# A two-layer decoder trunk: the written order inside the middle passes of its MLPs is changed

## The chip, the core and the metric

The kernel runs on one core of a Trainium2 chip. The metric is device time in microseconds (us). A core has engines with queues of their own: TensorE (PE in the profile, PEld for its weight loads) multiplies matrices, VectorE (DVE) and ScalarE (ACT) work on tiles element by element, GpSimd (POOL) and SyncE (SP) here only issue transfers. Matrix products land in PSUM, which has eight banks; everything else lives in SBUF.

## The reference

256 tokens of width 2048 pass through two layers. Layer 0 mixes with a short gated convolution, layer 1 with multi-head latent attention; each mixer is followed by a squared-ReLU MLP of inner width 8192, and every sub-layer ends in a layer norm:

```
def sq_relu_mlp(x, w1, w2):
    return jnp.square(jax.nn.relu(x @ w1)) @ w2
...
        h = layer_norm(ALPHA * h + mix, ln_g[layer, 0], ln_b[layer, 0])
        h = layer_norm(ALPHA * h + sq_relu_mlp(h, mlp_w1[layer], mlp_w2[layer]),
                       ln_g[layer, 1], ln_b[layer, 1])
```
All inputs and outputs are float32. The change concerns the two MLPs alone.

## The kernel before

Float32 products are made from two halves: `split` writes `hi`, a rounded copy of a tile (ACT, L139), and `lo`, what the rounding left out (DVE, L140). A product is hi x hi + hi x lo + lo x hi. So every weight tile that comes from memory (512 KB, `load_raw`, issued by SP) needs one ACT cast and one DVE subtraction before PE can use it.

An MLP (`mlp`) goes over the 8192 inner columns in eight passes `q` of 1024, and each pass over eight units `m` of 128 columns. Pass 0 is treated on its own. From pass 1 on a loop of **slots** runs, one slot for each unit (`steps`, L89). A slot holds:

- the **unit**: 16 x 2 matmuls of the first weight matrix (`mm_run`, L255 and L259) into one PSUM bank called "unit" (in slots without a pair, "6" by turns). Its sum is taken off by `evacuate`, which calls `whole`: an ACT copy (L399) and a DVE addition (L400) into the tile `fp`, which holds two units;
- in most slots the products of a **pair** of weight tiles of the second matrix with the hidden values of the pass before (`products_of`, `fast_products`): seven products by Strassen's scheme, 21 matmuls (L340 to L343) into the seven other banks.

After every odd unit two units are whole. ACT applies ReLU and square (L842), `form` makes three sums for the seven left factors (DVE, L688 to L691), and `finish_pair` splits the factors into hi and lo (tiles `h1a`, `h1c`, `h3a`, `h3c`). For the last unit of a pass, DVE does ReLU and square itself (L804). There is one `fp` tile, so a split must be done before the next even unit's sum is written.

Weights are prepared one slot ahead. `singles` are the two halves of the next unit's weights, one cast and one subtraction each. A pair is prepared in five steps by `prepare`: step 1 issues its two loads and makes `raw_t` (L172); step 2 splits the first tile; step 3 makes two differences (L177, L179) and splits `raw_t`; step 4 splits the second tile; step 5 splits the half-wide `t`. The function `step(i)` takes one of these steps for pair `i`.

The seven banks belong to one half `g` of the output columns at a time. After the fourth pair of a half (slot m=0 of the next pass) they change hands: seven **moves**, each an ACT copy out of a bank (`put_back`, L653) and mostly one back in (`resume`, L738). A slot that begins with moves still to make is called `crowded`; that is m=1. In pass 7 `fold` adds up parts of the output on DVE (L661).

The order of the work is the order in which the loop writes it: `Order.keep` chains all instructions of a slot on PE, on DVE and on ACT one behind the other, each engine for itself. Transfers are issued by SP in the order written and wait for one of seven `raw` buffers.

Before, a usual slot was written as: step 1, singles, step 2, step 3, products, `evacuate`, step 4, step 5, and behind an odd unit ReLU and square, sums and split. The split of units 0 and 1 stood in m=2 ahead of the products, that of the last two units between steps 4 and 5 of m=7.

Of the kernel before, what the change touches and what calls it, by code (L numbers as in the profile page):

```python
# [12 lines left out]
AF = mybir.ActivationFunctionType  # L13
# [3 lines left out]
P = 128  # L17
W = 256 + 2
T = 256
# [3 lines left out]
NQ = 8  # L23
QC = FF // NQ // P
# [12 lines left out]
FAST = range(1, NQ - 1)  # L37
SHIFT = 5
# [18 lines left out]
def trunk(ctx: ExitStack, tc: tile.TileContext, xT, vecs, lead, w_first, w_in, w_out, w_kv, w_q, w_uk, w_uv,  # L57
          w_qn, w_qp, w_o, w1, w2, w2f, cosT, sinT, mask, ident, gb, out):
    nc = tc.nc
# [53 lines left out]
    class Banks:  # L113
# [15 lines left out]
        @classmethod  # L129
        def next(cls):  # L130
            cls.count += 1
            return (cls.count - 1) % (4 if cls.more is None else 8)

    state = {"next": 0}
    ready = {}

    def split(hi, lo, src):

        nc.scalar.copy(hi, src)  # L139
        return nc.vector.tensor_tensor(lo, src, hi.bitcast(F32), ALU.subtract)  # L140
# [12 lines left out]
    def prepare(i):  # L153

        if len(stream[i]) == 1:
            raw = loaded.pop(i) if i in loaded else load_raw(i, stream[i][0])
            hi, lo = ready[i] = parts(i)
            split(hi, lo, tiled(raw))
            yield
            return  # L160
        r1, r2 = (load_raw(f"{i}_{j}", src) for j, src in enumerate(stream[i]))
        t = raws.tile([P, 1024], F32, tag="raw", name=f"raw{i}_t")
        out = []

        def finished(r, name):
            hi, lo = parts(name)
            split(hi, lo, tiled(r))
            out.append((hi, lo))

        b22, (b21, b12) = r1[:, BW:], (r2[:, :BW], r2[:, BW:])  # L170
        two = "p (a c) -> p a c"
        nc.vector.tensor_tensor(t.rearrange(two, a=2), b12.unsqueeze(1).to_broadcast([P, 2, BW]),  # L172
                                r1.rearrange(two, a=2), ALU.subtract)
        yield
        finished(r1, f"{i}_1")
        yield
        nc.vector.tensor_tensor(b12, b22, t[:, :BW], ALU.subtract)  # L177
        t4 = r1[:, :BW]
        nc.vector.tensor_tensor(t4, b21, b12, ALU.subtract)  # L179
        finished(t, f"{i}_t")  # L180
        yield
        finished(r2, f"{i}_2")
        yield
        f = state["fast"].tile([P, 2, BW], F32R, tag="t4", name=f"t4_{i}", bufs=2)
        split(f[:, 0, :], f[:, 1, :], t4)
        b1, t13, b2 = ([[v.rearrange("p b c -> p (b c)")[:, o:o + BW] for v in w] for o in (0, BW)] for w in out)
        ready[i] = {"11": b1[0], "22": b1[1], "21": b2[0], "T2": b2[1], "T1": t13[0], "T3": t13[1],
                    "T4": [f[:, 0, :], f[:, 1, :]]}
        yield

    def size(i):

        return 1 if len(stream[i]) == 1 else 5

    begun, loaded = {}, {}

    def step(i):

        steps = begun.setdefault(i, [prepare(i), 0])
        if steps[1] < size(i):  # L200
            next(steps[0])
            steps[1] += 1
# [373 lines left out]
    for k0, k1 in pieces:  # L576
        half, at = k0 // 8, slice(k0 % 8, (k1 - 1) % 8 + 1)
# [41 lines left out]
    def mlp(idx, ln, blocks, fast, begin=None, extra=None, last=False):  # L619
# [64 lines left out]
        def form(u):  # L684

            a21, a11, a12, s1, s2, s4 = (u[:, i * P:(i + 1) * P] for i in (0, 1, 3, 4, 6, 7))
            two = u.rearrange("p (i c) -> p i c", c=P)
            nc.vector.tensor_tensor(s1, a21, u[:, 2 * P:3 * P], ALU.add)  # L688
            nc.vector.tensor_tensor(two[:, 5:7, :], two[:, 0:5:4, :], a11.unsqueeze(1).to_broadcast([P, 2, P]),
                                    ALU.subtract)  # L690
            nc.vector.tensor_tensor(s4, a12, s2, ALU.subtract)  # L691

        def forms(u):

            if q in FAST or last:
                form(u)

        def finish_pair(j, u):
            f = factors[j // 2][:, j % 2]
            at = slice(P, 8 * P) if q in FAST else slice(0, 8 * P) if last else slice(0, 2 * T)  # L700
            split(f[:, 0, at], f[:, 1, at], u[:, at])

        q = 0
# [38 lines left out]
        rows = {}  # L742

        moves = []

        def move(n):

            for _ in range(n):
                if moves:
                    o, g, on = moves.pop(0)  # L750
                    put_back(o, g, ps[o])
                    if on:
                        resume(o, 1 - g)
# [14 lines left out]
        slots, i = [], state["next"]  # L768
        for q, m, pair in steps(last):
            n = (2 if q < NQ else 0) + (pair is not None)  # L770
            slots.append((q, m, pair, list(range(i, i + n))))
            i += n
        order = Order()
        for s, (q, m, pair, own) in enumerate(slots):
            lone = pair is None
            following = slots[s + 1][3] if s + 1 < len(slots) else []
            pairs = [i for i in following if size(i) > 1]
            ahead = [i for i in range(state["next"], (following or own)[-1] + 1) if i not in own and i not in begun]
            if not pairs:
                ahead = [i for i in range(state["next"], own[-1] + 6) if i not in own and i not in begun]  # L780
                ahead = ahead[:next((k for k, i in enumerate(ahead) if size(i) > 1), len(ahead))]
            singles = [i for i in ahead if size(i) == 1]
            for i in singles:
                loaded[i] = load_raw(i, stream[i][0])
            if q == FAST[0] and m == SHIFT:
                sums = act.tile([P, 4, 2, BW], F32, tag="xres", name=f"sums{idx}")
                for o, _, _ in FACTORS:
                    resume(o, 1)
            if q < NQ:
                w = take(2, 0)  # L790
                at = "6" if lone and (m - SHIFT) % 2 else "unit"
                un = psum("ps_u", bank[at])
                mm_run([(w, un)], xhl, 0, NC, NC, turned=TURNED if TURN(q, m) else None)

            def evacuate():

                if q == NQ:
                    return
                if m % 2 == 0:
                    rows[m // 2] = fast.tile([P, 8 * P], F32, tag="fp", name="fp")  # L800
                u = rows[m // 2]
                whole(un, u[:, (m % 2) * T:(m % 2 + 1) * T])
                if m == QC - 1:
                    nc.vector.scalar_tensor_tensor(u[:, T:2 * T], u[:, T:2 * T], 0.0, u[:, T:2 * T], ALU.max, ALU.mult)  # L804

            crowded = len(moves) > 0
            for i in pairs:
                step(i)
            for i in singles:
                step(i)  # L810
                move(1)
            if crowded:
                evacuate()
            for i in pairs:
                step(i)
            move(len(moves))
            for i in pairs:
                step(i)
            if rows and m == 2:
                finish_pair(0, rows.pop(0))  # L820
            if pair:
                products_of(*pair)
            if not crowded:
                evacuate()
            if q < NQ and m == QC - 1:
                forms(rows[m // 2])
            move(1)
            for i in pairs:
                step(i)
            move(1)  # L830
            if q < NQ and m == QC - 1:
                finish_pair(m // 2, rows.pop(m // 2))
            for i in pairs:
                step(i)
            move(2)
            if q < NQ:
                if m % 2 or m == QC - 2:
                    u = rows.get(m // 2)
                    if m < QC - 1:
                        at = u[:, :T] if m == QC - 2 else u[:, :2 * T]  # L840
                        for function in (AF.Relu, AF.Square):
                            nc.scalar.activation(at, at, function)  # L842
                        if m % 2:
                            forms(u)
                            if m > 1 or lone:
                                finish_pair(m // 2, rows.pop(m // 2))
                if extra and q == FAST[0] and m < NB:
                    for t in range(2):
                        extra(block, m, t, spare[1 + (2 * m + t) % 3])
                if begin and q == FAST[0] and m < 4 and m % 2 == 0:  # L850
                    nc.gpsimd.dma_start(parked[:, 4 * m:4 * m + 8, :], held_x[0][:, 4 * m:4 * m + 8, :])
                if q == NQ - 1 and m:
                    for _ in range(3 if m >= SHIFT else 2):
                        next(folds, None)
            order.keep()
        move(len(moves))
        for _ in folds:
            pass
# [436 lines left out]
```

## Time and profile before

| | us |
|---|---|
| median of three runs | 2048.57 (2048.47 to 2050.03) |
| the profiled execution | 2049.0 |
| its span, first to last instruction | 2047.2 |
| PE busy (11050 matmuls) | 2000.4 |
| DVE busy | 1757.3 |
| ACT busy | 1308.1 |
| slots of layer 0, first unit to the next stage | 452.1 to 1019.6 |
| slots of layer 1, first unit to the next stage | 1418.5 to 2015.8 |

Rows of the profile give start and length in us, the engine, the line of the kernel, the operation, and the tiles written and read. A bracket at the end of a row tells how long the engine was idle before it and what ended that. Rows of a window give its bounds, its length, the busy time of PE, PEld, DVE, ACT and POOL with the number of instructions, the granted clock of PE, the DMA share and GB/s. Rows of waits give the engine and line that waited, for whom, us in total, times, and the longest.

### The profile page before, as it was taken

Reading aid. Unit: us, or ns where it says so; the run is one execution under the profiler, and the core shown is the slowest. Engines: PE = TensorE matmul, PEld = TensorE weight load, DVE = VectorE, ACT = ScalarE, POOL = GpSimd, SP = SyncE. Lnnn points to the kernel's source line nnn. Section 1 sums busy time; section 2 is a strip of 40 time slices with the busy share of each in tenths; the row PEclk is TensorE's granted clock in tenths of the full one; section 3 lists DMA queues with packets and bytes.
Section 4 is the critical chain, followed back from the end, with each engine's and each line's share of the span. In section 5 each row is a group of like instructions: output and inputs, shape, how many; then the busy total and the mean of one; then the engine's idle time right before and its main releaser. Section 6 shows DMA issues by size and latency. Waiting matters only on the chain.

```text
span 2047.2 us, 29648 instructions
## 1 busy us (share of the span) xinstructions
PE 2000.4 (98%) x11050; PEld 1733.2 (85%) x11050; DVE 1757.3 (86%) x2539; ACT 1308.1 (64%) x1915; POOL 5.7 (0%) x27
## 2 busy tenths in 40 slices
PE   9999999999999999999999999999999999999998
PEld 8888888987887878888889998898788788887876
DVE  8667677777999999999898988776899999999998
ACT  7444455576767767677656665566676776767754
POOL 0000000000000000000000000000000000000000
PEclk9999999999999999999999999999999999999999
DMA  9766666664555556555665534664455555565554
GB/s 344 207 193 186 188 192 179 195 205 144 201 190 202 189 188 204 190 191 195 219 243 166 182 118 153 179 192 154 147 192 192 199 192 193 193 204 194 185 177 164
DMA packets 107711, 389.99 MB, mean 190 GB/s; under 512 B 11952, under 2 KB 12720, under 8 KB 107056
## 3 DMA queue, kind: packets, MB, share of 16 engines
q1 hardware_dynamic: 106560, 383.79, 57.5%
q0 software_dynamic: 864, 4.19, 0.5%
q8 instruction: 86, 1.41, 0.3%
q14 instruction: 57, 0.47, 0.1%
q10 hardware_dynamic: 144, 0.13, 0.0%
HBM read 383.87 MB, written 4.19 MB: 190 GB/s over the span
## 4 chain that ended last, share of the span: by engine, by line
PE 54%; DVE 33%; ACT 7%; issue 5%; DMA 1%; DVEq 0%; ACTq 0%
DVE lo L140 15%; PE ps_l L255 13%; PE ps_l L259 7%; PE ps_u L255 5%; DVE lo_t L140 4%; DVE raw_t L172 3%; PE ps_u L259 3%; ACT hi L139 3%; DVE raw L177 2%; DVE raw L179 2%; DVE t L140 2%; PE ps_d L342 2%; PE ps_d L343 2%; PE ps_d L340 2%; PE ps_w L289 2%
## 5 line engine op out<-in xcount | busy, mean ns | idle before, releaser
L140 DVE TENSOR_TENSOR lo<-raw,hi 128x1024 fp32r<-128x1024 f32 x710 | 848.2, 1220 | 133.3 <-ACT hi L139 61.3
L139 ACT CAST hi<-raw 128x1024 fp32r<-128x1024 f32 x710 | 725.0, 1050 | 258.9 <-PE ps_l L255 102.1
L255 PE MATMUL ps_u<-xhl,hi 128*128 128x512 f32 x1792 | 634.5, 400 | 38.3 <-DVE fp L400 38.3
L259 PE MATMUL ps_u<-xhl,lo 128*128 128x256 f32 x1792 | 489.6, 282 | 0.0
L255 PEld LDWEIGHTS ps_u<-xhl,hi 128*128 128x128 f32 x1792 | 333.4, 190 | 121.1 <-DVE fp L400 53.2
L259 PEld LDWEIGHTS ps_u<-xhl,lo 128*128 128x128 f32 x1792 | 342.6, 191 | 11.6
L255 PE MATMUL ps_l<-xhl_a,hi 128*128 128x512 f32 x704 | 244.1, 393 | 0.0
L259 PE MATMUL ps_l<-xhl_a,lo 128*128 128x256 f32 x704 | 195.4, 279 | 0.0
L255 PEld LDWEIGHTS ps_l<-xhl_a,hi 128*128 128x128 f32 x704 | 132.1, 188 | 29.9
L259 PEld LDWEIGHTS ps_l<-xhl_a,lo 128*128 128x128 f32 x704 | 131.9, 188 | 0.2
L139 ACT CAST hi_t<-raw_t 128x1024 fp32r<-128x1024 f32 x100 | 105.1, 1051 | 41.9 <-DVE raw_t L172 41.2
L172 DVE TENSOR_TENSOR raw_t<-raw,raw 128x1024 f32<-128x1024 f32 x100 | 121.9, 1219 | 0.2 <-DMA raw<-in_w2f_dram 0.2
L140 DVE TENSOR_TENSOR lo_t<-raw_t,hi_t 128x1024 fp32r<-128x1024 f32 x100 | 121.9, 1219 | 0.0
L399 ACT COPY t<-ps_u 128x256 f32<-128x256 f32 x112 | 41.3, 369 | 110.2 <-PE ps_u L259 110.2
L255 PE MATMUL ps_l<-z,hi 128*128 128x512 f32 x240 | 82.4, 391 | 0.0
L842 ACT ACTIVATE fp<-fp 128x512 f32<-128x512 f32 (+1 forms) x112 | 64.9, 580 | 26.5 <-DVE fp L400 24.7
L400 DVE TENSOR_TENSOR fp<-ps_u,t 128x256 f32<-128x256 f32 x112 | 47.0, 420 | 35.7 <-ACT t L399 34.4
L289 PE MATMUL ps_w<-xd,hi 128*128 128x258 f32 x256 | 72.8, 284 | 0.0
L288 PE MATMUL ps_w<-xd,lo 128*128 128x258 f32 x256 | 72.3, 282 | 0.0
L287 PE MATMUL ps_w<-xd,hi 128*128 128x258 f32 x256 | 72.3, 282 | 0.0
L179 DVE TENSOR_TENSOR raw<-raw 128x512 f32<-128x512 f32 x100 | 69.2, 692 | 3.5
L255 PE MATMUL ps_l<-oT,hi 128*128 128x512 f32 x208 | 71.3, 391 | 0.0
(361 smaller groups left out, 3900.0 us busy)
## 6 DMA issues: line engine op xcount, KB each, us to landing
raw<-in_w_dram SPq DMA_DIRECT2D x312, 512.0 KB, 4.2
raw<-in_w2f_dram SPq DMA_DIRECT2D x200, 512.0 KB, 4.3
raw<-in_w_in_dram SPq DMA_DIRECT2D x88, 512.0 KB, 4.4
raw<-in_w_out_dram SPq DMA_DIRECT2D x32, 512.0 KB, 4.3
raw<-in_w_o_dram SPq DMA_DIRECT2D x32, 512.0 KB, 4.2
raw<-in_w_kv_dram SPq DMA_DIRECT2D x10, 512.0 KB, 6.0
raw<-in_w_q_dram SPq DMA_DIRECT2D x8, 512.0 KB, 4.0
raw<-in_w_uk_dram SPq DMA_DIRECT2D x8, 512.0 KB, 4.3
```

The lines of the kernel that those rows point to most:

```text
L139: nc.scalar.copy(hi, src)
L140: return nc.vector.tensor_tensor(lo, src, hi.bitcast(F32), ALU.subtract)
L172: nc.vector.tensor_tensor(t.rearrange(two, a=2), b12.unsqueeze(1).to_broadcast([P, 2, BW]), r1.rearrange(two, a=2), ALU.subtract)
L179: nc.vector.tensor_tensor(t4, b21, b12, ALU.subtract)
L255: nc.tensor.matmul(ps, w[blk // 8][0][:, blk % 8, :], x, start=first, stop=False)
L259: nc.tensor.matmul(ps[:, :T], w[blk // 8][1][:, blk % 8, :], x[:, :T], start=False, stop=last)
L287: nc.tensor.matmul(ps[:, :W], hi, x[k][:, :W], start=k == 0, stop=False)
L288: nc.tensor.matmul(ps[:, :W], lo, x[k][:, :W], start=False, stop=False)
L289: nc.tensor.matmul(ps[:, :W], hi, x[k][:, W:], start=False, stop=k == NC - 1)
L399: nc.scalar.copy(t, ps[:, T:])
L400: nc.vector.tensor_tensor(out, ps[:, :T], t, ALU.add)
L842: nc.scalar.activation(at, at, function)
```

## The change

It touches the loop of slots only.

- `evacuate` comes ahead of step 3: a usual slot is now written as step 1, singles, (products), step 2, `evacuate`, step 3, step 4, step 5.
- Splits of factors are put on a list `due` and written in the next slot, behind its first single (or behind step 1 where there are no singles). For the last two units of a pass the three sums stand right behind `evacuate`. What is left on the list is written after the loop.
- Moves: one behind each of `evacuate`, step 3, step 4 and step 5; in a crowded slot all that are left stand ahead of step 2.
- Before the first pair: in the last slot but two ahead of it (`far`, slot m=3 of pass 1) steps 1 to 3 of that pair are written at the slot's end.
- In pass 7 the folds are taken five to a slot from m=5 on (layer 0), or one to a slot from m=1 on (layer 1).

```
-        def finish_pair(j, u):
+        def finish_pair(j, u, of):
             f = factors[j // 2][:, j % 2]
-            at = slice(P, 8 * P) if q in FAST else slice(0, 8 * P) if last else slice(0, 2 * T)
+            at = slice(P, 8 * P) if of in FAST else slice(0, 8 * P) if last else slice(0, 2 * T)
             split(f[:, 0, at], f[:, 1, at], u[:, at])
...
-        order = Order()
+        order, due = Order(), []
+
+        def split_due():
+
+            while due:
+                j, of = due.pop()
+                finish_pair(j, rows.pop(j), of)
+
         for s, (q, m, pair, own) in enumerate(slots):
             lone = pair is None
             following = slots[s + 1][3] if s + 1 < len(slots) else []
             pairs = [i for i in following if size(i) > 1]
-            ahead = [i for i in range(state["next"], (following or own)[-1] + 1) if i not in own and i not in begun]
-            if not pairs:
-                ahead = [i for i in range(state["next"], own[-1] + 6) if i not in own and i not in begun]
-                ahead = ahead[:next((k for k, i in enumerate(ahead) if size(i) > 1), len(ahead))]
-            singles = [i for i in ahead if size(i) == 1]
+            far = slots[s + 2][3][-1:] if s + 2 < len(slots) and not pairs and lone else []
+            far = [i for i in far if size(i) > 1]
+            end = following[-1] + 1 if pairs else far[0] if far else own[-1] + 6
+            singles = [i for i in range(state["next"], end) if i not in own and size(i) == 1 and i not in begun]
...
+            def to_step(n):
+
+                for i in pairs:
+                    while i not in begun or begun[i][1] < n:
+                        step(i)
+
             def evacuate():
...
                 if m == QC - 1:
                     nc.vector.scalar_tensor_tensor(u[:, T:2 * T], u[:, T:2 * T], 0.0, u[:, T:2 * T], ALU.max, ALU.mult)
+                    forms(u)
+                    due.append((m // 2, q))
 
             crowded = len(moves) > 0
-            for i in pairs:
-                step(i)
+            to_step(1)
+            if not singles:
+                split_due()
             for i in singles:
                 step(i)
                 move(1)
+                split_due()
             if crowded:
                 evacuate()
-            for i in pairs:
-                step(i)
-            move(len(moves))
-            for i in pairs:
-                step(i)
-            if rows and m == 2:
-                finish_pair(0, rows.pop(0))
+                move(len(moves))
+            hi_first = pairs and not crowded and q < NQ
+            to_step(1 if hi_first else 2)
             if pair:
                 products_of(*pair)
             if not crowded:
+                if hi_first:
+                    for i in pairs:
+                        step(i)
                 evacuate()
-            if q < NQ and m == QC - 1:
-                forms(rows[m // 2])
             move(1)
-            for i in pairs:
-                step(i)
+            to_step(3)
             move(1)
-            if q < NQ and m == QC - 1:
-                finish_pair(m // 2, rows.pop(m // 2))
-            for i in pairs:
-                step(i)
-            move(2)
+            to_step(4)
+            move(1)
+            to_step(5)
+            move(1)
             if q < NQ:
-                if m % 2 or m == QC - 2:
-                    u = rows.get(m // 2)
-                    if m < QC - 1:
-                        at = u[:, :T] if m == QC - 2 else u[:, :2 * T]
-                        for function in (AF.Relu, AF.Square):
-                            nc.scalar.activation(at, at, function)
-                        if m % 2:
-                            forms(u)
-                            if m > 1 or lone:
-                                finish_pair(m // 2, rows.pop(m // 2))
+                if m % 2 and m < QC - 1 or m == QC - 2:
+                    u = rows[m // 2]
+                    at = u[:, :T] if m == QC - 2 else u[:, :2 * T]
+                    for function in (AF.Relu, AF.Square):
+                        nc.scalar.activation(at, at, function)
+                    if m % 2:
+                        forms(u)
+                        due.append((m // 2, q))
...
-                if q == NQ - 1 and m:
-                    for _ in range(3 if m >= SHIFT else 2):
+                if q == NQ - 1:
+                    for _ in range((m > 0) if last else 5 if m >= SHIFT else 0):
                         next(folds, None)
+                for i in far:
+                    for _ in range(3):
+                        step(i)
             order.keep()
+        split_due()
         move(len(moves))
```

## The prediction

> **What bounds the kernel now.** I read the page first, then the waits of TensorE, then single stretches, then the timelines of one pass.
>
> ```profile
> span 2047.2 us, 29648 instructions
> PE 2000.4 (98%) x11050; PEld 1733.2 (85%) x11050; DVE 1757.3 (86%) x2539; ACT 1308.1 (64%) x1915; POOL 5.7 (0%) x27
> ...
> PE 54%; DVE 33%; ACT 7%; issue 5%; DMA 1%; DVEq 0%; ACTq 0%
> ```
> TensorE (PE) is busy for 98% of the span, yet a third of the chain that ended last runs through VectorE (DVE). In the list of PE's waits one row is large, and all of it lies in the middle passes:
>
> ```profile
> PE ps_u L255 <- DVE fp L400: 38.3, 32, 4.1
> ```
> A unit's first matmul waits until L400 has read the sum of the unit before it, since both use the one bank "unit". How long a slot takes without that wait is seen in the timeline of PE:
>
> ```profile
> 689.01 0.39 PE L255 MATMUL ps_u<-xhl,hi 128*128 128x512 f32 x1
> ...
> 694.58 0.39 PE L340 MATMUL ps<-hi,h1a 128*128 128x512 f32 x1
> ...
> 699.38 0.42 PE L255 MATMUL ps_u<-xhl,hi 128*128 128x512 f32 x1
> ```
> A unit takes 5.57, its pair's products 4.80, together 10.37; a slot without a pair 5.57. The two stretches that the change touches (the second from its last slot without a pair on) are these, with their length right behind the window:
>
> ```profile
> 452.10:1019.60 567.50, 550.26 (x2802) 464.37 (x2801) 515.26 (x619) 396.50 (x533) 0.00 (x0) 0.99 0.57 189
> 1444.20:2015.84 571.64, 550.58 (x2760) 462.76 (x2758) 536.13 (x646) 401.42 (x532) 0.00 (x0) 0.99 0.58 191
> ```
> The first holds 48 slots with a pair and 8 without: 48 x 10.37 + 8 x 5.57 = 542.3, so 25.2 is lost. The second holds 51 with, 1 without and one pair alone: 528.9 + 5.6 + 4.8 = 539.3, lost 32.3. All that this change can win is these 57.5 us; the PE column (550) understates it, since stretched matmuls count as busy.
>
> Who loses it is seen in one pass, by its window and its waits:
>
> ```profile
> 602.50:689.00 86.50, 83.89 (x425) 70.41 (x424) 81.14 (x98) 61.80 (x82) 0.00 (x0) 1.00 0.59 195
> ...
> DVE lo L140 <- ACT hi L139: 2.3, 3, 0.9
> ...
> DVE h1a L140 <- ACT h1a L139: 1.1, 1, 1.1
> DVE h1c L140 <- ACT h1c L139: 1.1, 1, 1.1
> ```
> Eight slots should take 83.0 of PE; they take 86.5. DVE works 81.1 and waits for ScalarE (ACT) for 4.5: 2.3 behind the weight halves and 2.2 behind the factor splits. 81.1 + 4.5 is nearly the whole pass: a pass is set by DVE's work and DVE's waits, and PE's waits are how it shows.
>
> **DVE's order, from the timeline, and what a slot costs.**
>
> ```profile
> 605.27 1.22 DVE L172 TENSOR_TENSOR raw_t<-raw,raw 128x1024 f32<-128x1024 f32 x1
> 606.41 3.49 DVE L140 TENSOR_TENSOR lo<-raw,hi 128x1024 fp32r<-128x1024 f32 x3
> 609.82 0.69 DVE L177 TENSOR_TENSOR raw<-raw,raw_t 128x512 f32<-128x512 f32 x1
> 610.54 0.69 DVE L179 TENSOR_TENSOR raw<-raw 128x512 f32<-128x512 f32 x1
> 611.15 1.22 DVE L140 TENSOR_TENSOR lo_t<-raw_t,hi_t 128x1024 fp32r<-128x1024 f32 x1
> 612.28 0.42 DVE L400 TENSOR_TENSOR fp<-ps_u,t 128x256 f32<-128x256 f32 x1
> 612.62 1.22 DVE L140 TENSOR_TENSOR lo<-raw,hi 128x1024 fp32r<-128x1024 f32 x1
> 613.75 0.68 DVE L140 TENSOR_TENSOR t<-raw,t 128x512 fp32r<-128x512 f32 x1
> 614.35 1.22 DVE L172 TENSOR_TENSOR raw_t<-raw,raw 128x1024 f32<-128x1024 f32 x1
> ...
> 626.29 0.28 DVE L688 TENSOR_TENSOR fp<-fp 128x128 f32<-128x128 f32 x1
> ...
> 627.28 1.22 DVE L172 TENSOR_TENSOR raw_t<-raw,raw 128x1024 f32<-128x1024 f32 x1
> ...
> 648.76 1.09 DVE L140 TENSOR_TENSOR h1c<-fp,h1c 128x896 fp32r<-128x896 f32 x1 [1.06 <-ACT h1c L139]
> 649.77 1.22 DVE L172 TENSOR_TENSOR raw_t<-raw,raw 128x1024 f32<-128x1024 f32 x1
> ```
> From start to start: L172 and each lo 1.14, L177 0.72, L179 0.61, L400 0.34, the last t 0.60: a slot 9.08. The three sums of L688 to L691 add 0.99 and a split 1.01. A pass has four of each: 8 x 9.08 + 4 x 2.00 = 80.6, and 0.5 for L804.
>
> **The edits, one by one.** *L400 ahead of L177, L179 and lo_t*: DVE reaches it 0.72 + 0.61 + 1.14 = 2.5 earlier. *A split one slot later, behind the first lo*: The sums that it reads are then a slot old, and ACT makes its half while DVE does L172 and lo, so the 1.1 of waiting goes (2.2 a pass, where slots m=3 and m=5 end). A slot with a split now costs 10.09, one with sums 10.07, both below PE's 10.37; before they alternated between 9.08 and 11.1 plus the wait. If that cover were gone, the same 1.1 would stand in the next slot. *Loads*: SP's queue keeps its order, since the singles are still issued ahead of the pair; a pair's second load still goes out behind the second lo and has 5.6 (609.9 to the next slot's L172) for
>
> ```profile
> raw<-in_w2f_dram SPq DMA_DIRECT2D x200, 512.0 KB, 4.3
> ```
> which leaves 1 us. I take nothing for it; if the cover failed, L172 would come late by the rest. POOL's two stores and PE's order do not move.
>
> *The moves* (L653 and L738, seven per pass, on ACT) are spaced anew: three instead of two lie ahead of the last cast of m=0, and in m=1 the seventh goes ahead of the cast of the pair's first half, which DVE waits for. The prices in ACT's timeline:
>
> ```profile
> 610.54 1.05 ACT L139 CAST hi<-raw 128x1024 fp32r<-128x1024 f32 x1 [0.35 <-DVE raw L177]
> 611.50 0.57 ACT L653 COPY sums<-ps 128x512 f32<-128x512 f32 x1
> ...
> 612.63 0.62 ACT L139 CAST t<-raw 128x512 fp32r<-128x512 f32 x1
> ```
> A cast 0.96, a move 1.13 (611.50 to 612.63), the small cast 0.5.
>
> **A pass after the change, walked slot by slot** (times from the start of the slot's unit; "lag" is when DVE begins the slot's L172).
>
> m=0, lag 3.1: the split of m=7's sums now stands here. It ends at 3.1 + 1.14 + 1.14 + 1.09 = 6.5; the third matmul of the products reads it and is due at 5.57 + 0.46 = 6.0. PE waits **0.5**, in every pass, where it did not wait before.
>
> m=0 to m=1: ACT can begin to move when the first product is done, 7.05 (6.07, three matmuls of 0.23, 0.3 to land). From there it never rests: seven moves 7.9, four casts 3.8, the small cast 0.5, the unit's copy 0.3, so the cast of the pair's first half begins at 19.6 and ends at 20.6, which is 9.8 in m=1 (10.87 long m=0). DVE then has 1.14 + 0.72 + 0.61 + 1.14 + 1.14 + 0.60 + 0.99 = 6.3 left: m=2 starts with a lag of 5.8. ACT makes DVE wait 3.7 here, against 2.3.
>
> m=2: L172, lo, split, lo, lo, then L400 at 5.8 + 5.6 = 11.4, done at 11.8. The next unit wanted 10.37: PE waits **1.5**. Before:
>
> ```profile
> 635.96 0.50 PE L255 MATMUL ps_u<-xhl,hi 128*128 128x512 f32 x1 [2.11 <-DVE fp L400]
> ```
> m=3 to m=7: lags 4.0, 3.7, 3.5, 3.2, 2.9; L400 is done by 9.8 at the latest. No wait; the 0.5 of m=4 and of m=6 go. m=7 adds 0.5: lag 3.1 again, so this repeats.
>
> So a pass is 83.0 + 0.5 + 1.5 = **85.0**, against 86.5. Walked the same way, the order of before gives 86.3; I add 1 us in all for what the walk leaves out.
>
> *Start of the pairs* (q=1). PE's row and DVE's row before:
>
> ```profile
> 493.68 0.42 DVE L400 TENSOR_TENSOR fp<-ps_u,t 128x256 f32<-128x256 f32 x1
> ...
> 494.15 0.50 PE L255 MATMUL ps_u<-xhl,hi 128*128 128x512 f32 x1 [3.71 <-DVE fp L400]
> ```
> DVE is packed from the first pair on, so beginning that pair two slots ahead only refills the 1.1 that the split no longer waits; with the 2.5 of the order L400 comes at 493.7 - 1.1 - 2.5 = 490.1, and PE waits **0.4** (0.8 in the second layer). Then lag 4.9: L400 of m=6 ends 0.7 too late (**0.75**), and in m=0 of q=2 the split ends at 7.6: **1.6**. In q=2 four of the moves reload nothing, so ACT is freer and no wait is left in m=2.
>
> *Last pass, first layer*: no sums, folds only from m=5 on: 0.5 + 0.1. *Last pass, second layer*: one fold (0.60) a slot and wider splits: **2.3** in m=2, **0.8** in m=4 and in m=6. Then the tail. Before, the last split was ready for the last pair:
>
> ```profile
> 2009.98 1.22 DVE L140 TENSOR_TENSOR h3a<-fp,h3a 128x1024 fp32r<-128x1024 f32 x1
> ```
> Now it waits for the next slot's first lo. From m=7's L400 (6.9): 0.45 + 0.46 + 0.99 + 0.72 + 0.61 + 1.14 + 1.14 + 0.60, fold 0.60, lo 1.14, split 1.22: 16.0, against 10.83 where PE wants it: **5.1** with PE idle, and all of PE's work to the end lies behind it.
>
> **The clock.** Two windows of before, and a third with a like wait:
>
> ```profile
> 806.20:809.60 3.40, 1.29 (x7) 0.78 (x6) 3.30 (x5) 3.40 (x5) 0.00 (x0) 1.00 0.27 107
> 809.60:813.05 3.45, 3.45 (x13) 2.86 (x12) 3.45 (x5) 1.50 (x2) 0.00 (x0) 0.51 0.54 142
> ...
> 632.10:635.50 3.40, 1.75 (x8) 1.13 (x6) 3.26 (x5) 2.96 (x4) 0.00 (x0) 1.00 0.56 201
> ```
> With PE busy for 1.29 of 3.40 the granted clock fell to 0.51 for the next 3.45, which costs 1.7; with 1.75 busy it stayed at 1.00. So waits of 1.5 are safe, 2.3 seldom not, and the 5.1 of the tail brings one such stretch: **1.7**. [...]
>
> **The sum.** First layer 0.4 + 0.75 + 1.6 + 4 x 2.0 + 0.6 = 11.4; second 0.8 + 0.75 + 1.6 + 8.0 + 0.5 + 2.3 + 1.6 + 5.1 + 1.7 = 22.3; 1 for the rest: 34.7. Saved 57.5 - 34.7 = 22.8. The profiled execution took 2049.0, so 2026.2; the median shown is 0.4 lower, so **2026**. Ends of the forecast: no new waits for the split and no clock fall, 2016; waits of 2.3 left in m=2, splits 1.0 late, two clock stretches, 2038.
>
> **The rivals.** *PE's own floor.* If ACT's moves did not hold DVE (a pass 83.0), all but the start and the tail would go: 57.5 - 12 = 45 saved, 2003. For it: DVE's 81.1 is below 83.0. Against: ACT's row of moves is full in both orders. Chance 0.11. *The split ahead of its reader.* In m=0 the products read a split that now stands right before them. It decides from a lag of 2.6 on; every us above costs one us in twelve passes and the tail. To lose it needs a lag above 5.2 (2.1 x 13 = 27 more); at 5.7 it gives 2060. For it: ACT must deliver two casts first, and lags of 4 to 6 do occur. Against: slots m=3 to m=7 each win 0.3 back. Chance 0.11. *Nothing moves*: DVE's waits return elsewhere (ACT 3.7 instead of 2.3, the splits at the tail) to the same sum, 2045 to 2051. Chance 0.05.
>
> **How the numbers follow.** Forecast 0.73 at 2026. The range 2008 to 2038 holds the forecast's own ends and the nearer half of the floor's case. About 0.2% (4 us) is what a measurement here can tell: faster 0.83, same 0.06, slower 0.11.
>
> **What would show it.** Right: the waits for L400 fall from 38.3 to about 17; no DVE wait of 1.1 for a factor split; new waits of PE's products for a split, about 0.5 in each m=0 and 5 after the last unit; passes of 85.0; lo behind the seventh move waiting 1.7 in each m=1. Wrong: passes of 83 (floor) or 87 and more with products waiting over 2 (split), or L172 waiting for loads.

## The result, and the profile after

The changed kernel takes 2025.39 us (median of 4 runs, 2024.01 to 2027.43) against 2049.3 us; the ratio is 0.9884, with a 95% interval of 0.9867 to 0.9901. The forecast was 2026. The profiled execution of after took 2027.43, the longest of the four, and has a span of 2025.6, 21.6 less than that of before.

The page of after:

```profile
PE 1993.8 (98%) x11050; PEld 1731.1 (85%) x11050; DVE 1754.5 (87%) x2539; ACT 1298.8 (64%) x1915; POOL 5.6 (0%) x27
...
PE 49%; DVE 37%; issue 7%; ACT 6%; DMA 0%; DVEq 0%; ACTq 0%
```
and in the list of its waits:

```profile
PE ps_u L255 <- DVE fp L400: 12.6, 12, 1.9
```
The busy shares say next to nothing (DVE 86% before, 87% after). The row that carried the 38.3 now has 12.6, in 12 waits instead of 32. DVE's share of the chain that ended last has grown from 33% to 37%, but this says little too: in e2 below, which takes nearly the same time, it is 17%.

Where the time came from is seen by cutting both spans at the same four points: the start of the first layer's loop, its end, the second layer's last slot without a pair, and the end of the second layer's last unit. Before (its first stretch, 567.50, stands in the prediction):

```profile
1019.60:1444.20 424.60, 422.96 (x2739) 387.06 (x2738) 353.42 (x706) 256.28 (x464) 2.70 (x5) 1.00 0.54 172
1444.20:2006.40 562.20, 541.14 (x2718) 455.02 (x2717) 526.83 (x634) 392.66 (x520) 0.00 (x0) 0.99 0.57 190
2006.40:2047.20 40.80, 35.06 (x147) 27.01 (x145) 35.69 (x60) 16.84 (x26) 0.00 (x0) 0.98 0.43 156
```
and after:

```profile
452.10:1005.50 553.40, 545.54 (x2802) 462.35 (x2801) 511.22 (x615) 392.72 (x533) 0.00 (x0) 1.00 0.59 194
1005.50:1433.85 428.35, 424.57 (x2739) 388.25 (x2738) 356.18 (x710) 255.21 (x464) 2.69 (x5) 1.00 0.55 171
1433.85:1979.10 545.25, 535.17 (x2718) 452.17 (x2717) 521.19 (x629) 387.31 (x519) 0.00 (x0) 1.00 0.59 194
1979.10:2025.60 46.50, 37.44 (x147) 28.03 (x145) 39.80 (x65) 18.06 (x27) 0.00 (x0) 0.96 0.43 155
```
The number right behind each window is its length. The two loops win 14.1 and 16.95; the stretch between them gives back 3.75 and the end 5.7: 21.6 in all. Of the 31 that the loops win, 20.5 are waits of PE (38.3 for L400 before; 12.6 for L400 and 5.2 for a factor split after). Another 8.5 is clock: by the clock records of the two traces, the loops of before hold six stretches of 3.41 us at half clock, those of after one, and each costs 1.7. One pass of after, by its window:

```profile
596.80:681.65 84.85, 83.46 (x426) 70.53 (x425) 80.92 (x98) 61.08 (x83) 0.00 (x0) 1.00 0.61 197
```
and by rows of DVE's timeline in it, then of PE's:

```profile
602.03 1.09 DVE L140 TENSOR_TENSOR h1a<-fp,h1a 128x896 fp32r<-128x896 f32 x1
617.34 1.23 DVE L140 TENSOR_TENSOR lo<-raw,hi 128x1024 fp32r<-128x1024 f32 x1 [1.67 <-ACT hi L139]
625.94 1.09 DVE L140 TENSOR_TENSOR h1c<-fp,h1c 128x896 fp32r<-128x896 f32 x1
```

```profile
602.57 0.40 PE L342 MATMUL ps<-lo,h1a 128*128 128x512 f32 x1
603.17 0.50 PE L343 MATMUL ps<-hi,h1a 128*128 128x512 f32 x1 [0.21 <-DVE h1a L140]
...
629.69 0.50 PE L255 MATMUL ps_u<-xhl,hi 128*128 128x512 f32 x1 [1.18 <-DVE fp L400]
```
84.85 instead of 86.50. The splits at 602.03 and 625.94 have no bracket: DVE finds ACT's half ready, where it waited 1.1 before. The price is at 603.17: the third matmul of the products starts 0.60 behind the second instead of 0.23. `lo` at 617.34 waits 1.67 behind the seventh move, and two slots later unit m=3 starts late.

### The profile page after: what moved, and what is told of

It is laid out like the page before. It is cut to its first block, busy times and chain, and to the rows that moved or that the text cites. A ratio compares the mean times of both kernels' runs of the same rounds, so it can differ in the third digit from the quotient of the medians.

```text
span 2025.6 us, 29534 instructions
## 1 busy us (share of the span) xinstructions
PE 1993.8 (98%) x11050; PEld 1731.1 (85%) x11050; DVE 1754.5 (87%) x2539; ACT 1298.8 (64%) x1915; POOL 5.6 (0%) x27
## 4 chain that ended last, share of the span: by engine, by line
PE 49%; DVE 37%; issue 7%; ACT 6%; DMA 0%; DVEq 0%; ACTq 0%
DVE lo L140 13%; PE ps_l L255 13%; PE ps_l L259 7%; DVE lo_t L140 5%; DVE raw_t L172 4%; PE ps_u L255 3%; DVE raw L179 3%; DVE raw L177 3%; DVE t L140 2%; PE ps_d L343 2%; PE ps_d L342 2%; PE ps_d L340 2%; ACT hi L139 2%; PE ps_w L289 2%; PE ps_w L288 2%
## 5 line engine op out<-in xcount | busy, mean ns | idle before, releaser
L255 PE MATMUL ps_u<-xhl,hi 128*128 128x512 f32 x1792 | 624.3, 395 | 12.7 <-DVE fp L400 12.6
L172 DVE TENSOR_TENSOR raw_t<-raw,raw 128x1024 f32<-128x1024 f32 x100 | 121.9, 1219 | 0.0
L400 DVE TENSOR_TENSOR fp<-ps_u,t 128x256 f32<-128x256 f32 x112 | 47.2, 421 | 35.3 <-ACT t L399 35.3
L179 DVE TENSOR_TENSOR raw<-raw 128x512 f32<-128x512 f32 x100 | 69.2, 692 | 3.5
L140 DVE TENSOR_TENSOR t<-raw,t 128x512 fp32r<-128x512 f32 x100 | 68.6, 686 | 3.5 <-ACT t L139 3.5
```

What stands on the lines that cost most here:

```text
L255: nc.tensor.matmul(ps, w[blk // 8][0][:, blk % 8, :], x, start=first, stop=False)
L400: nc.vector.tensor_tensor(out, ps[:, :T], t, ALU.add)
```

## Which part of the change brings the gain

Two theories: the gain is the late split (DVE no longer stands still for ACT), or it is L400's earlier place (the bank is free 2.5 sooner). The first run takes the late split away and keeps all else; the second does the late split alone; the third leaves out the early begin of the first pair.

**e1_split_in_own_slot**, the changed kernel with:

```
-            if not singles:
-                split_due()
...
-                split_due()
...
+            if due:
+                to_step(2)
+                split_due()
...
+            if m == QC - 1:
+                split_due()
...
+                        if m > 1 or lone:
+                            split_due()
```
The first two pieces take the split from behind the first single; the others put it where it stood before: in m=2 ahead of the products, in m=7 in its own slot, in m=3 and m=5 behind the sums.

> The changed kernel with one part undone: the splits of the factors stand where they stood before (m=3 and m=5 behind their sums in the same slot, m=1 one slot later behind the second cast, m=7 in its own slot). L400 stays ahead of L177, L179 and lo_t, and the moves and folds stay as changed. Theory S (the late split is what brings the gain; the earlier L400 brings nothing by itself, since DVE is packed and the 1.1 us waits for ScalarE come back): passes of 87.0, waits of 1.1 in front of the splits again, L400 late again where m=3 and m=5 end, time 2045 to 2050, no gain left. Theory O (the bank is free 2.5 us earlier, and that is the gain): passes stay at 85 to 85.5 and the time at 2025 to 2031.

Measured: 2069.53 us, ratio 1.0096 (1.0079 to 1.0113): slower than before, and outside both forecasts: S had no gain at all, but no loss. One pass of it, and the 3.4 us right behind PE's long wait in that pass:

```profile
607.60:696.00 88.40, 84.76 (x426) 71.83 (x425) 81.13 (x98) 61.20 (x82) 0.00 (x0) 0.98 0.56 191
637.10:640.50 3.40, 3.40 (x11) 2.88 (x11) 3.40 (x4) 1.99 (x3) 0.00 (x0) 0.50 0.39 110
```
and the waits of the pass:

```profile
PE ps_u L255 <- DVE fp L400: 3.6, 1, 3.6
...
DVE h1c L140 <- ACT h1c L139: 1.1, 1, 1.1
DVE h1a L140 <- ACT h1a L139: 1.1, 1, 1.1
```
The waits of 1.1 are back, as theory S said, and PE loses some 3.7 a pass, about the 4.0 that makes passes of 87.0. But it loses them in one piece (m=2), where before lost 2.1 and several times 0.5, and after this one piece the granted clock is 0.50 for 3.4 us: 1.7 more, in the pass shown and in most others (five stretches of it in each layer's loop). The mean clock of this execution is 0.991 against 0.995 of before. So the wait was priced right, and the clock behind it was left out. Without the late split the rest of the change, the earlier L400 with it, brings no gain: theory O falls. (The new places of the moves stay in this run too; the earlier L400 entirely by itself was not run.)

**e2_only_late_split**, the kernel before with:

```
             for i in singles:
                 step(i)
                 move(1)
+                split_due()
...
-            if rows and m == 2:
-                finish_pair(0, rows.pop(0))
...
-                finish_pair(m // 2, rows.pop(m // 2))
+                due.append((m // 2, q))
...
-                            if m > 1 or lone:
-                                finish_pair(m // 2, rows.pop(m // 2))
+                            due.append((m // 2, q))
```


> The kernel before with one part of the change done alone: every factor split one slot later behind the first lo; order of L400, moves, folds and first pairs as before. Theory S: passes of 84.9 (even a little shorter than with the whole change), time 2027 to 2031. Theory O: L400 stays behind L177, L179 and lo_t, so passes of 86 to 86.5 and a time of 2043 to 2049.

Measured: 2027.91 us, ratio 0.9891 (0.9876 to 0.9905), which overlaps that of the whole change. A pass of it and its end, by windows, and PE's wait for the last split:

```profile
605.60:690.40 84.80, 83.24 (x427) 70.66 (x426) 80.95 (x98) 61.87 (x82) 0.00 (x0) 1.00 0.60 201
1984.20:2026.50 42.30, 35.34 (x147) 26.98 (x145) 35.74 (x60) 16.76 (x26) 0.00 (x0) 1.00 0.42 151
```

```profile
PE ps L343 <- DVE h3a L140: 1.3, 1, 1.3
```
84.80: the late split alone makes the pass. What the rest of the change wins elsewhere in the loops (they are 557.1 and 574.2 long here, by their first and last unit, against 553.5 and 570.9) it gives back for the most part at the end, which takes 42.3 here and 46.5 with the whole change.

**e3_no_far**, the changed kernel with:

```
-                for i in far:
-                    for _ in range(3):
-                        step(i)
```


> The changed kernel with the first pair of each layer begun one slot ahead, not two. The prediction's step (DVE is packed there, the early begin brings nothing): within 1 us of the changed kernel, 2024 to 2027. Rival (the early begin is what took the first wait for L400 from 3.7 to 0.4): a wait of 2 to 3.5 us at the first pair of each layer, 2029 to 2032.

Measured: 2025.98 us, ratio 0.9882 (0.9868 to 0.9897); in the first layer's loop the unit's waits are 5.1 in all, against 5.2. Beginning the pair two slots ahead does nothing that can be measured.

## What holds the pass at 85

**e4_half_before_move7**, the changed kernel with:

```
                 evacuate()
+                move(len(moves) - 1)
+                to_step(2)
                 move(len(moves))
```


> The changed kernel with one move fewer in DVE's way: in the slot whose moves are under way (m=1) the cast of the pair's first half is written ahead of the seventh move instead of behind it. Theory A (ScalarE's moves hold DVE, and the 1.3 left at the end of m=2 is that wait handed on): lo in m=1 waits 0.6 instead of 1.7, the wait of unit m=3 falls from 1.35 to about 0.3, passes of 83.9, 11 us saved in all: 2014. Rival D (DVE's own work sets the pass, and ScalarE's order only shifts where it waits; the seventh move now makes the products of the second half wait for its bank): passes stay at 85, 2023 to 2028.

**e5_split7_in_slot**, the changed kernel with:

```
             to_step(3)
             move(1)
+            if m == QC - 1:
+                split_due()
             to_step(4)
```


> The changed kernel with the split of m=7 alone put back into its own slot (behind the pair's lo_t); the splits of m=1, 3 and 5 stay one slot later. Theory T (the products that wait for the split of m=7 cost 0.4 in each m=0, and the split behind the last unit costs its idle time and the stretch of half clock behind it): passes of 84.5, no 0.4 in m=0, PE's loss behind the last unit down from 7.9 to about 2, time 2013 to 2016. Rival (m=7 now takes 1.0 more of DVE, so L400 of m=2 comes as much later and the wait of unit m=3 grows by what m=0 gave up): passes stay at 85.0, only the end of the second layer wins, 2019 to 2021.

**e6_both**, with both edits:

> The changed kernel with the split of m=7 in its own slot and the cast of the pair's first half ahead of the seventh move. Theory: the two gains are of different waits and add up: passes of 83.3 to 83.4, 2002 to 2004. Rival (they are the same slack of DVE, counted twice): passes of 83.9, 2008 to 2011.

Measured: e4 2014.32 us, ratio 0.9824 (0.9810 to 0.9839); e5 2020.39, 0.9853 (0.9840 to 0.9867); e6 2008.26, 0.9794 (0.9781 to 0.9807). A pass of e4, DVE's wait for ACT in it, and a pass of e6:

```profile
686.30:770.10 83.80, 83.57 (x426) 70.50 (x425) 81.00 (x98) 61.01 (x82) 0.00 (x0) 1.00 0.59 201
```

```profile
DVE lo L140 <- ACT hi L139: 1.6, 3, 0.9
```

```profile
689.60:772.90 83.30, 83.30 (x426) 70.52 (x425) 80.91 (x98) 61.06 (x83) 0.00 (x0) 1.00 0.59 202
```
e4 hits its forecast: the wait of 1.67 for the cast is gone (0.85 is the longest left), with it the wait of unit m=3. One cast moved ahead of one move in ACT's order, where ACT is busy for 64% of the span, is worth 11 us, because DVE stands behind it and PE behind DVE. In e5 the products of m=0 wait no more (its loops are 3.6 shorter each), but the end takes 48.3, not less: theory T is right for the passes and wrong for the end, and the time comes out as the rival had it, though not for the rival's reason. e6 adds the two in the passes, 83.30 against a floor of 83.0, as its theory had it. Its time, 2008.26, is 4 us above the theory's 2002 to 2004 and lies where the rival had it, again not for the rival's reason (passes of 83.9): the gain that was expected at the end did not come, the end takes 47.6.

## What is given back behind the loops

**e7_folds_from_2**, the changed kernel with:

```
-                    for _ in range((m > 0) if last else 5 if m >= SHIFT else 0):
+                    for _ in range((m > 0) if last else 5 if m >= SHIFT else int(m > 1)):
```


> The changed kernel with three of the sixteen folds of the first layer moved from the end of its loop to m=2, 3 and 4 of the last pass. Theory F (the 3.8 that the first layer's gain of 14.1 loses behind its loop is a chain: last fold, release of the buffer, load of xback, its first mean; and the half clock after that wait): last fold 3 to 4 us earlier against the loop's end, PE's wait for xback from 3.8 to about 0.5, no fall of the clock there, 2020 to 2022. Rival (the load of xback takes its 7 us because the weight loads crowd it, whenever it starts, and PE has to wait for it all the same): within 1 us of the changed kernel, 2024 to 2027.

**e8_all_three**, e6 with the same edit:

> All three at once: the split of m=7 in its own slot, the cast ahead of the seventh move, three folds earlier. If they add up: 1996 to 1999. If the earlier folds only fill the slack that the other two need in the last pass: 2001 to 2004.

Measured: e7 2023.74 us, ratio 0.9872 (0.9858 to 0.9885), between its two forecasts and not told apart from the change (0.9867 to 0.9901); e8 2010.86, 0.9807 (0.9794 to 0.9820), no better than e6, its median 2.6 above, and above both of its forecasts. The first mean of `xback` in the timeline of PE, before and after:

```profile
1033.64 0.70 PE L454 MATMUL mu0p<-xback,ones 128*128 128x256 f32 x2 [1.62 <-DVE xback L452]
```

```profile
1022.14 0.93 PE L454 MATMUL mu0p<-xback,ones 128*128 128x256 f32 x2 [3.76 <-DVE xback L452]
```
and in e7, e8 and e6:

```profile
1017.17 0.70 PE L454 MATMUL mu0p<-xback,ones 128*128 128x256 f32 x2
```

```profile
1011.43 0.70 PE L454 MATMUL mu0p<-xback,ones 128*128 128x256 f32 x2 [1.92 <-DVE xback L452]
```

```profile
1014.59 0.70 PE L454 MATMUL mu0p<-xback,ones 128*128 128x256 f32 x2 [2.27 <-DVE xback L452]
```
The two links between the last fold and that mean, in after:

```profile
1014.72 1.63 POOL L880 DMA_DIRECT2D xback<-parked  x3 [0.25 <-DVE acc L661]
...
1021.80 0.29 DVE L452 TENSOR_SCALAR xback<-xback 128x256 f32<-128x256 f32 x1 [3.91 <-DMA xback<-parked]
```
In the trace of after the chain is as theory F has it: the last fold ends late, `xback` is loaded into the buffer that it frees, and PE waits 3.76 instead of 1.62, then runs at half clock for 3.4 us (1.7): 3.8 more than before, the 3.75 given back. In e7's trace that wait is gone: the load begins 5.7 behind the last unit instead of 9.1, and it takes 4.9 from its issue to L452 instead of 7.1. Why the load itself is shorter is not shown. In e8 the same edit leaves 1.92 and a fall of the clock, and in e3, e4, e5 and e12, which have the folds of after here, PE waits 2.55, 2.96, 2.78 and 2.46, with a fall of the clock in all but e3. So the chain is seen, but its cost changes from trace to trace: the stretch between the loops is 1.2 to 2.9 longer than before in these four, and 3.75 in after. That these folds can be placed for a gain that a median shows is not shown.

At the end three runs take a piece away: **e10_no_last_folds** (`if p == FAST[-1] and not last:` ahead of the last layer's folds) and **e11_last_stats_first** (the four `scaled(...)` of the finished half written behind the other half's statistics; in the trace three of them stand there) start from e6, **e12_two_folds** (`2 * (m > 0)` for `(m > 0)`) from the changed kernel.

> The kernel with both edits (the split of m=7 in its own slot, the cast ahead of the seventh move), and the eight folds of L661 of the second layer left out, so that one half of the second layer's sums is not put together; VectorE has 4.8 us less to do in the last pass. Theory V (in the last pass and behind it VectorE is what PE waits for): the waits of 0.75, 0.62 and 0.50 for L400 in m=3, 5 and 7 go, and VectorE comes 1.2 to 2 earlier to the end: 2003 to 2006. Rival E (the end is held by the written order of the last normalisation on VectorE, four additions of L1182 ahead of the last L1171, and by PE's wait for the last weights): only the 1.9 of the waits goes and the end keeps its 4.1 for umeans: 2006 to 2007.

> The kernel with both edits, and at the very end of the program three of the four additions of L1182 (the finished half of the output) behind the last L1171 on VectorE instead of ahead of it. Theory E (the earlier end of the loop meets a VectorE order that puts 2.7 us of additions ahead of the statistics on which PE's last products hang): PE's wait for umeans from 4.1 to about 2, without the half clock behind it: 2004 to 2006. Rival V (VectorE has the same work to the end in either order): 2007 to 2009.

> The changed kernel with the eight folds of the second layer two to a slot (m=1 to m=4 of the last pass) instead of one to a slot with the last one behind the loop, so that VectorE has two folds fewer to do around and behind the last unit. Theory F (the time from the last unit to the end, 46.5 against 40.8 before, is long because VectorE still has folds to do there, and not because of the late split alone): this stretch 43 to 45, while the loop gets up to 2 us longer where two folds a slot stand in PE's way (m=2 to m=5): 2022 to 2026. Rival S (the stretch is long because the split of the last sums stands behind the next slot's first lo): stretch unchanged at 46 to 47, loop longer, 2026 to 2029.

Measured: e10 2002.95 us, ratio 0.9765 (0.9751 to 0.9778), eight folds left out; e11 2004.83, 0.9774 (0.9761 to 0.9788), the whole computation; e12 2026.30, 0.9876 (0.9860 to 0.9892), no different from the change. PE's waits in the end of e6:

```profile
PE ps L1195 <- ACT umeans L1192: 4.1, 1, 4.1
PE ps_e L340 <- ACT hi L139: 1.7, 1, 1.7
```
The ends of e10, of e11 with its wait, and of e12:

```profile
1957.10:2001.20 44.10, 35.88 (x147) 26.72 (x145) 37.65 (x62) 17.76 (x27) 0.00 (x0) 1.00 0.43 156
```

```profile
1957.70:2003.00 45.30, 37.35 (x147) 27.26 (x145) 39.23 (x65) 17.98 (x27) 0.00 (x0) 0.96 0.44 160
```

```profile
PE ps L1196 <- ACT umeans L1193: 2.1, 1, 2.1
```

```profile
1979.40:2024.50 45.10, 37.57 (x147) 28.10 (x145) 38.31 (x63) 18.01 (x27) 0.00 (x0) 0.96 0.44 160
```
In e11 PE's wait falls as theory E had it, 4.1 to 2.1, and its end is 2.3 shorter, though the clock still falls once there: the order of the last instructions, and not PE, set e6's end. e10 shows that DVE's work does so too: its end is 3.5 shorter without the folds, more than theory E allowed. Its two waits there are 0.8 and 3.2 (1.7 and 4.1 in e6), and the clock, 0.95 in e6's end, stays at 1.00. e12 falls between its two forecasts: its end is 1.4 shorter and its loop 1.6 longer (572.6), so folds moved about on DVE are only paid for elsewhere. e11 is the best whole kernel here, 1.1% below the change by the ratios (0.9774 / 0.9884 = 0.989).

**e9_folds_on_pool**, both edits of e6 and:

```
-                nc.vector.tensor_tensor(d, a, b, ALU.add)
+                nc.gpsimd.tensor_tensor(d, a, b, ALU.add)
...
-                    for _ in range((m > 0) if last else 5 if m >= SHIFT else 0):
+                    for _ in range(4 if m else 0):
```


> The kernel of the run with both edits (the split of m=7 in its own slot, the cast ahead of the seventh move), and all folds of L661 (sixteen in the first layer, eight in the second) on GpSimd instead of VectorE, up to four in each slot from m=1 of the last pass on. No trace so far shows such an addition on GpSimd; its memset of 128x512 took 0.53 us, so an estimate of 1 to 2 us for one fold. Theory V (VectorE's backlog is what is left at the ends of both layers): no wait for xback behind the first layer (2.3 before), the waits for L400 of about 0.8 in m=3, 5 and 7 of the second layer's last pass gone, VectorE with 1.2 less to do behind the last unit: 2000 to 2003. Rival P (GpSimd and VectorE get into each other's way, or a fold takes so long that the release of the buffer comes later than on VectorE): VectorE's additions longer than their 0.60 to 1.14 while GpSimd works, PE waiting for xback by 3 and more, 2008 to 2016.

Up to four folds a slot also means that in the first layer the second half's folds are written ahead of the last moves of its sums, so that half is not put together as in the reference; the instructions are the same in number. Measured: 2016.41 us, ratio 0.9839 (0.9825 to 0.9852): 8 us slower than with the folds on DVE. GpSimd's timeline in the first layer's last pass, DVE's there, and the window of the slot m=2, then that of e6:

```profile
945.30 2.01 POOL L661 TENSOR_TENSOR sums<-sums 128x512 f32<-128x512 f32 x1 [0.23 <-ACT sums L653]
947.39 2.16 POOL L661 TENSOR_TENSOR acc<-acc,sums 128x512 f32<-128x512 f32 x1
949.51 1.75 POOL L661 TENSOR_TENSOR sums<-sums 128x512 f32<-128x512 f32 x1
...
984.51 1.30 POOL L661 TENSOR_TENSOR acc<-acc,sums 128x512 f32<-128x512 f32 x1 [25.37 <-ACT sums L653]
```

```profile
946.18 0.43 DVE L400 TENSOR_TENSOR fp<-ps_u,t 128x256 f32<-128x256 f32 x1
...
950.14 1.67 DVE L179 TENSOR_TENSOR raw<-raw 128x512 f32<-128x512 f32 x1
951.73 2.31 DVE L140 TENSOR_TENSOR lo_t<-raw_t,hi_t 128x1024 fp32r<-128x1024 f32 x1
...
960.15 1.21 DVE L140 TENSOR_TENSOR lo<-raw,hi 128x1024 fp32r<-128x1024 f32 x1
```

```profile
949.10:964.60 15.50, 10.54 (x54) 8.61 (x52) 15.46 (x12) 7.59 (x11) 10.05 (x6) 1.00 0.40 111
```

```profile
949.50:959.90 10.40, 10.40 (x55) 8.87 (x54) 10.37 (x13) 8.13 (x12) 0.00 (x0) 1.00 0.61 193
```
Rival P holds: while GpSimd adds, most additions of DVE with both operands in SBUF take 1.0 to 1.1 more (2.31 for 1.21, 1.67 for the 0.69 of L179), and a fold of the first layer takes 1.74 to 2.27 where the first one of a quiet stretch takes 1.30. The slot takes 15.5 instead of 10.4. What P had of the buffer did not come: it is released in time, and no wait for `xback` is left.

## Why the prediction was right, point by point

- **What bounds it** (PE behind DVE, DVE behind its own work and ACT): right. The pass went from 86.5 to 84.85 for 85.0 forecast, with the forecast waits at the forecast places: products of m=0 0.4 late (0.5), `lo` behind the seventh move 1.67 (1.7), unit m=3 1.2 idle (1.5), no wait for a factor split (2.2 a pass before). e4 shows the handing on, ACT to DVE to PE, by taking its first link away. The sign "from 38.3 to about 17" came out lower, at 12.6.
- **L400 ahead of L177, L179 and lo_t** stood first among the edits, with 2.5 us. By e1 and e2 it is not what shortens a pass: e2 has the pass without it, and e1 has no gain with it. The walk had the right sum because it counted DVE's work, which is the same in any order.
- **Start of the pairs**: that the early begin brings nothing itself was right (e3).
- **Last pass, second layer**: the wait in m=2 was 1.92 by the profile (2.3 forecast), but then the clock fell, as the text held possible and the sum did not count, and the two waits of 0.8 behind it did not come: that DVE caught up while PE ran at half clock is argued. Forecast 2.3 + 1.6, measured 1.9 + 1.7.
- **The tail**: 6.8 forecast, 5.7 measured; the size was near and the way it comes about was not. PE's waits in the end of after:

```profile
PE ps_e L340 <- ACT hi L139: 1.8, 1, 1.8
PE ps L1191 <- ACT umeans L1188: 1.6, 1, 1.6
PE ps_e L342 <- DVE lo L140: 1.1, 1, 1.1
PE ps L340 <- ACT h3a L139: 0.5, 1, 0.5
```
Before has the 1.6 for `umeans` alone. So 3.4 of waiting came in, and one stretch at half clock (1.7). The walk of DVE's work was right: the split of m=7's sums ended 16.2 behind the start of its unit, for 16.0 forecast. But PE does not stand idle for 5.1 until then. It takes other products first, waits there for a cast, a subtraction and ACT's half of the split, and reads DVE's half without a wait. With the late split alone (e2) PE waits 1.3 for it and the end is 1.5 longer than before; with the split back in its slot and all else as changed (e5) the end is 48.3, longer still, with 4.1 for `umeans`. The step that failed is "all of PE's work to the end lies behind it": what DVE and ACT have left to do behind the loop sets the end, with the split there or not. e12 puts 1.4 on the folds that the change leaves there; that the rest is L177, L179 and lo_t (0.72 + 0.61 + 1.14), now behind the last L400, is argued, not shown.
- **Behind the first layer**: the sum had nothing there, and 3.75 was given back. The change leaves one fold behind the loop; the forecast walked the loop to its end and did not ask what waits for the last fold.
- **The sum**: forecast 13.8 + 16.8 - 6.8 - 1 = 22.8; measured 14.1 + 16.95 - 5.7 - 3.75 = 21.6 in the profiled executions, 23.9 by the medians. That 2026 and 2025.39 lie so close is in part luck. Behind the first layer 3.75 was missing, and the tail, set 1.1 too high, and the 1 for the rest made up for some of it. In the loops, too, two errors met: the first layer's loop was to lose 11.4 in waits and lost 7.8 (5.2 for L400, 2.6 for splits), but it is 11.1 above its floor of 542.3 all the same, since the floor is too low: e6's passes take 83.3, not 83.0, without a wait of PE.
- **The rivals**: PE's floor was out of reach of this change for the reason given (the moves); with that reason gone and the split of m=7 back, e6's passes come to 83.3. "The split ahead of its reader costs more" did not happen: the lag behind which it decides stayed near 3.
- **Loads**: the margin for L172 held; no row of L172 waits for one.
- **Clock**: that a long wait brings a stretch of 1.7 was right (behind 3.76 for `xback` in after and behind 3.6 in e1 the granted clock is 0.50 for 3.4). That waits of 1.5 are safe and waits of 2.3 seldom does not follow from its two windows: both hold part of a wait of 2.11 (the one that ends at 635.96 and the one that ends at 809.06), only placed otherwise in the window, and 1.92 in the last pass was followed by a fall. PE's busy time in them, 1.75 and 1.29, tells more than the length; see the last section.

## What to carry to other kernels

When an engine is packed, reordering its work moves its waits but wins only the time in which it stood still for another; look for those rows first, and price an edit by them. Walk a change past the end of the loop: what frees a buffer, what is written behind the last unit, and who waits there. A wait in one piece can cost half as much again as the same wait in several (3.6 and then 1.7 in e1), so look at the granted clock behind each.

## What the runs showed of the hardware that was not expected

Whether the clock falls behind a wait is not settled by its length: of the waits for `xback` above, 1.92 in e8 was followed by a fall and 2.27 in e6 was not. In the records it goes with where the wait lies. By the traces' clock records, which give each change of the granted clock, a stretch at half clock lasts 3.41 us or twice that, but for the last one of a run. In each of the fourteen traces the beginnings of two such stretches lie a whole multiple of 3.413 us apart: in after they are at 1022.48, 1930.43 and 1988.45, which are 266 and 17 such lengths. So each trace can be cut into windows of 3.413 us, counted from one of its falls, and the other falls lie on edges of these windows. The window that holds e8's wait and the one behind it, then the two that share e6's wait:

```profile
1009.26:1012.67 3.41, 1.49 (x8) 1.06 (x7) 1.59 (x3) 0.39 (x2) 0.54 (x1) 1.00 1.00 383
1012.67:1016.08 3.41, 3.41 (x10) 2.64 (x9) 3.41 (x7) 1.04 (x1) 0.00 (x0) 0.50 1.01 394
```

```profile
1009.90:1013.31 3.41, 2.42 (x11) 1.68 (x9) 1.92 (x2) 1.05 (x1) 0.39 (x1) 1.00 0.92 290
1013.31:1016.72 3.41, 2.13 (x9) 1.80 (x10) 2.41 (x5) 0.37 (x1) 0.54 (x1) 1.00 1.00 353
```
e6's longer wait is cut in two by an edge, PE is busy for 2.42 and 2.13 on its two sides, and the clock stays at 1.00. Over all fourteen traces, the first 30 us and the last two windows of each left out, the 42 falls from full clock came behind windows in which PE was busy for 1.63 us or less; of the windows at full clock with so little, only two (1.49 in e11, 1.53 in e1) were not followed by one. That is a count over these traces; what sets the clock is not shown by them.

While GpSimd added in e9, most additions of DVE with both operands in SBUF took 1.0 to 1.1 us more (2.31 for 1.21), and a fold of the first layer took 1.74 to 2.27 beside them, for 1.30 undisturbed. The additions in which DVE reads from PSUM did not grow: L400 at 946.18 took its usual 0.43 while a fold was under way, and those at 984.35 and 993.24, which met one too, took 0.42. Why the two kinds differ is not shown.
